# One product between the two forms of each weight sum in the last projection

## The chip, the cores and the metric

The kernel runs on one core of a Trainium2 chip (trn2). A core has a matrix engine (TensorE, in the profile PE, with PEld for its weight loads), a vector engine (VectorE, DVE), an activation engine (ScalarE, ACT), a general engine (GpSimd, POOL) and an engine that mostly issues transfers (SyncE, SP). Each engine works through its own list of instructions in order, and they wait for each other by semaphores. The metric is the device time of one execution in microseconds (us), lower is better.

## The reference, cut to what matters

Two layers on 512 tokens of width 1024. Only the end of the second layer and the final norm bear on the change:

```
def mla_layer(x, cos, sin, norm_g, w_in, ..., w_out):
    ...
    o = causal_mla_attention(q_nope, q_rope, k_nope, k_rope, v)
    y = o.reshape(B, S, MLA_WIDTH) * jax.nn.silu(z)      # 512 x 2048
    return x + y @ w_out                                 # w_out 2048 x 1024
...
    return rmsnorm(x, final_norm)
```

All is float32, and the sums must be accurate to that.

## The kernel before

Every product of two float32 matrices is made of three matmuls: both operands are split into a high and a low half, and `mm3` (lines 181 to 185) adds high x high (L183), then one low x high (L184) and the other (L185). The high half is an ACT copy (L166, L188, L559), the low half a DVE subtraction that reads the high one (L167, L189, L560).

The last projection, y @ w_out, is cut in 2 x 2 blocks and done by the scheme of Strassen and Winograd, with seven block products in place of eight. The gated attention result `y` is cut by tokens and by rows of the contraction into `a11, a12, a21, a22` (each 128 partitions x 8 x 256), the weights by contraction half (0 or 1) and by columns (`LEFT`, `RIGHT`). A product has 48 matmuls of 128 x 512: two strips of the weight block (`q` = 0, 1), two token tiles (`t` = 0, 1), four blocks of the contraction (`k`), three matmuls each. `multiply` goes through q, then t, then k.

The weight sums are made in place, by transfers that add to what lies there. `x_sum` has eight tiles `b_x` of 256 KB, `y_sum` four tiles `b_y` of 512 KB. A plain load is issued by SP (L548), an adding one by POOL (L546). `strip(i)` splits one half of the tiles into `w_hi` and `w_lo`. There are four buffers for those, so two strips at a time. An adding load into a tile can be issued only after the `w_lo` that reads the tile's old content.

The token side of a product goes into one of two slots: `slots[0]` is `a_hi_5948` and `a_lo_5949` in the rows below, `slots[1]` is `a_hi_5551` and `a_lo_5552`. `split_rows` fills a slot in two halves, `combine_rows` (L1055) adds or subtracts blocks of `y`, two DVE instructions per half.

The products collect in three pairs of PSUM banks: `acc` (`bank_5573`, `bank_5574`), `both` (`bank_6038`, `bank_6039`) and `last` (`bank_6040`, `bank_6041`). `gather` (L610, on DVE) adds a bank to the residual `xs`. A product that goes on in a bank can start only when the gather has read it. I name the products by their strips:

| product | token side | weight side | banks |
|---|---|---|---|
| first half | a11 | half 0, LEFT, a plain strip | acc |
| t1 | s1 = a21 - a22 | half 0, LEFT + RIGHT (`x_sum`) | both |
| p2 | a12 | half 1, LEFT (`y_sum`) | last |
| t2 | s2 = s1 - a11 | t1's sum + half 1, RIGHT (`x_sum`) | acc, going on |
| y1 | s2 + a12 | half 1, RIGHT (`y_sum`, a plain load) | both, going on |
| y2 | s3 = a11 - a21 | y1's block + half 0, RIGHT (`y_sum`) | acc, going on |
| t4 | a22 | t2's sum + half 1, LEFT (`x_sum`) | acc, going on |

The first of them runs between the last heads of the attention. `products()` writes out the order of t1 to y2 by hand, and `finish()` that of t4, the squares for the final norm (L1219 on ACT, `total` and `power` on POOL) and the stores. In both, `tc.manual_schedule()` keeps the order of the code on every engine.

Of the kernel before, what the change touches and what calls it, by code (L numbers as in the profile page):

```python
# [15 lines left out]
ALU = mybir.AluOpType  # L16
# [34 lines left out]
def trunk_kernel(  # L51
# [41 lines left out]
    def bank(dtype=F32):  # L93
        return ps.tile([P, 512], dtype, name="bank", tag="bank")
# [92 lines left out]
    def halves(src, hi, lo):  # L187
        act.activation(hi, src, AF.Copy)  # L188
        dve.tensor_tensor(lo, src, f32(hi), ALU.subtract)  # L189
# [51 lines left out]
    def start():  # L241
# [85 lines left out]
        for k in range(4):  # L327
            ready(0, k)
            products(0, k)
        w_lo(0, 4, 2)  # L330
        w_lo(1, 4, 2)
        ready(0, 4)
        products(0, 4)
        square(2)
        power(2)
        ready(0, 5)
        products(0, 5)
        ready(0, 6)
        scale(2)
# [194 lines left out]
    LEFT, RIGHT = slice(0, 512), slice(512, D)  # L534
# [35 lines left out]
    def quarters():  # L570

        return [
            [
                y[:, half * 8 + 2 * i : half * 8 + 2 * i + 2, t * 256 : (t + 1) * 256]
                for i in range(4)
            ]
            for t in range(2)
            for half in range(2)
        ]
# [9 lines left out]
    def part(o, wv, slot, q, t, start, stop, more, c=whole_row):  # L589

        for k in range(4):
            mm3(
                o,
                tuple(v[:, 4 * q + k, t * P : (t + 1) * P] for v in slot),
                tuple(v[:, k, c] for v in wv),
                start and k == 0,
                stop and k == 3,
                more=more,
            )

    def multiply(banks, strips, slot, start, then=None):
        for q in range(2):
            for t in range(2):
                part(banks[t], strips[q], slot, q, t, start and q == 0, q == 1, not start)
                if then and q == 1:
                    then(t)

    def gather(t, c, b, op=ALU.add):

        dve.tensor_tensor(xs[:, t, c], xs[:, t, c], b, op)  # L610


    a11, a12, a21, a22 = quarters()

    slots = [tuple(v[:, :, s * 256 : (s + 1) * 256] for v in (h_hi, h_lo)) for s in range(2)]
# [7 lines left out]
    x_sum, y_sum = Summed(w_out, 2), Summed(w_out, 2)  # L623
# [7 lines left out]
    acc = [bank() for _ in range(2)]  # L631
# [7 lines left out]
    both = [bank() for _ in range(2)]  # L639
# [23 lines left out]
    last = [bank() for _ in range(2)]  # L663
# [367 lines left out]
    def values(h):  # L1031
# [17 lines left out]
    a11, a12, a21, a22 = (  # L1049
        y[:, half * 8 : half * 8 + 8, t * 256 : (t + 1) * 256] for t in range(2) for half in range(2)  # L1050
    )

    def combine_rows(out, a, b, op, k0, k1):
        for k in range(k0, k1, 2):
            dve.tensor_tensor(*(v[:, k : k + 2, :] for v in (out, a, b)), op)  # L1055

    def split_rows(src, slot, k0, k1):
        halves(*(v[:, k0:k1, :] for v in (src, *slot)))
    x_sum, y_sum = Summed(w_out2, 1), Summed(w_out2, 2)
# [38 lines left out]
    first_half, slots = {}, {}  # L1098
    for h in range(H):
        p, odd = divmod(h, 2)  # L1100
        g, t = divmod(h + 5, 4)
        if h == 12:
# [3 lines left out]
            acc = [bank() for _ in range(2)]  # L1106
# [47 lines left out]
    s3, s2 = a21, a11  # L1154
    second_sum((("pt_hi", 1), ("pt_lo", 1)))
    both = [bank() for _ in range(2)]
    last = [bank() for _ in range(2)]
    g_fin = row(final_norm, D, "g_fin", tag="gain")

    def products():  # L1160

        combine_rows(s1, a21, a22, ALU.subtract, 6, 8)
        split_rows(s1, slots[0], 6, 8)
        x_sum.load(1, RIGHT, add=True, pieces=range(4))
        t1.append(x_sum.strip(1))
        x_sum.load(1, RIGHT, add=True, pieces=range(4, 8))
        multiply(both, t1, slots[0], True)
        split_rows(a12, slots[1], 0, 4)
        p2 = [y_sum.strip(0)]
        split_rows(a12, slots[1], 4, 8)  # L1170
        combine_rows(s3, a11, a21, ALU.subtract, 6, 8)
        combine_rows(s2, s1, a11, ALU.subtract, 6, 8)
        for t in range(2):
            gather(t, LEFT, acc[t])
        p2.append(y_sum.strip(1))
        y_sum.load(1, RIGHT)
        multiply(last, p2, slots[1], True)
        split_rows(s2, slots[0], 0, 4)
        split_rows(s2, slots[0], 4, 8)
        for t in range(2):  # L1180
            gather(2 + t, RIGHT, both[t])
        t2 = x_sum.strips()
        x_sum.load(1, LEFT, add=True)
        multiply(acc, t2, slots[0], False)
        for i in (0, 4):
            combine_rows(s2, s2, a12, ALU.add, i, i + 4)
            split_rows(s2, slots[1], i, i + 4)
        y1 = [y_sum.strip(0)]
        for t in range(2):
            gather(t, LEFT, last[t])  # L1190
        y1.append(y_sum.strip(1))
        y_sum.load(0, RIGHT, add=True)
        multiply(both, y1, slots[1], False)
        for t in range(2):
            gather(t, RIGHT, acc[t], ALU.subtract)
        split_rows(s3, slots[0], 0, 4)
        split_rows(s3, slots[0], 4, 8)
        for t in range(2):
            square(t, LEFT)
            total(t)  # L1200
        y2 = [y_sum.strip(0)]
        for t in range(2):
            gather(t, RIGHT, both[t])
        y2.append(y_sum.strip(1))
        for t in range(2):
            square(t, RIGHT)
            power(t)
        multiply(acc, y2, slots[0], False)
        split_rows(a22, slots[1], 0, 4)
        split_rows(a22, slots[1], 4, 8)  # L1210
# [6 lines left out]
    def square(t, c):  # L1217
        r = sm.tile([P, 1], F32, name="ssq", tag="ssq8", bufs=12)
        act.activation(  # L1219
            junk[:, : c.stop - c.start], xs[:, t, c], AF.Square, scale=D**-0.5, accum_out=r  # L1220
        )
        ssq[t].append(r)

    def total(t):

        r = sm.tile([P, 1], F32, name="total")
        pool.tensor_scalar(r, ssq[t][0], EPS, None, ALU.add)
        for q in ssq[t][1:]:
            pool.tensor_tensor(r, r, q, ALU.add)
        ssq[t] = [r]  # L1230

    def power(t):

        rs[t] = sm.tile([P, 1], F32, name="rs")
        pool.tensor_tensor(rs[t], ssq[t][1], ssq[t][0], ALU.add)
        pool.tensor_tensor(rs[t], rs[t], mhalf, ALU.pow)
# [92 lines left out]
```

## Time and profile before

| | |
|---|---|
| median of 3 runs | 716.93 us (716.78 to 717.99) |
| the profiled execution's own time | 715.48 us |
| its span in the profile | 713.6 us, so 1.9 us lie around it |
| PE busy | 700.9 us (98%) |
| DVE, ACT, POOL busy | 444.4, 347.5, 137.5 us |
| mean granted TensorE clock | 0.998 |
| t1 begins, the span ends | 639.25 us, 713.6 us |

The times in the rows are microseconds from the span's start. A row of the timeline has start, duration, engine, line, operation, output <- input, form and count, and in brackets how long the engine had been idle before it and what ended that. A matmul's end is modelled and overlaps the next one, so what counts is the distance from one start to the next.

### The profile page before, as it was taken

How to read it: one execution, taken by the hardware profiler on the slowest of the kernel's cores; microseconds unless marked ns; L12 is line 12 of the kernel's file. 1: busy time of each engine (PE TensorE's matmuls, PEld its weight loads, DVE VectorE, ACT ScalarE, POOL GpSimd, SP SyncE). 2: the span in 40 equal slices, each digit the busy share in tenths (PEclk: the TensorE clock that was granted, in tenths of full speed). 3: DMA queues.
4: the chain of work that ended last, by engine and by line, in shares of the span. 5: the costliest groups of instructions: out<-in, count | busy, mean ns of one | idle time of the engine just before them, and what ended most of it. 6: DMA issues, size and time to landing. Idle time of an engine off the chain costs nothing.

```text
span 713.6 us, 10044 instructions
## 1 busy us (share of the span) xinstructions
PE 700.9 (98%) x3529; PEld 600.6 (84%) x3529; DVE 444.4 (62%) x866; ACT 347.5 (49%) x748; POOL 137.5 (19%) x182
## 2 busy tenths in 40 slices
PE   8999999999999999999999999999999999999986
PEld 7988888888888888789888888898989898988875
DVE  5963452572486897750644220686676777699875
ACT  6452331341344465553652324756475477456662
POOL 5000000000001251064600006212221130122621
PEclk9999999999999999999999999999999999999999
DMA  8342323333245997334333433214122264378943
GB/s 259 105 144 73 118 83 94 104 84 108 89 148 144 235 192 136 96 86 129 99 117 103 118 97 101 78 27 108 52 65 70 79 163 132 65 172 212 153 84 119
DMA packets 69475, 82.79 MB, mean 116 GB/s; under 512 B 12080, under 2 KB 45872, under 8 KB 69424
## 3 DMA queue, kind: packets, MB, share of 16 engines
q1 hardware_dynamic: 60384, 65.10, 30.4%
q0 software_dynamic: 8896, 16.78, 13.8%
q8 instruction: 28, 0.46, 0.3%
q10 hardware_dynamic: 144, 0.26, 0.1%
q14 instruction: 23, 0.19, 0.1%
HBM read 75.83 MB, written 2.10 MB: 109 GB/s over the span
## 4 chain that ended last, share of the span: by engine, by line
PE 94%; DMA 2%; DVE 1%; issue 1%; ACT 1%; POOL 0%; POOLq 0%; SPq 0%; ACTq 0%; DVEq 0%
PE bank L184 28%; PE bank L183 28%; PE bank L185 28%; PE bank L1022 2%; PE bank L301 2%; PE bank L986 1%; PE bank L985 1%; DMA b_y<-in_mla_w_out 1%; PE bank L226 1%; PE bank L271 1%; PE bank L988 0%; PE bank L1044 0%; DMA xs<-in_x 0%; ACT junk L1219 0%; DVE a_lo L189 0%
## 5 line engine op out<-in xcount | busy, mean ns | idle before, releaser
L166 ACT ACTIVATE w_hi<-raw 128x512 fp32r<-128x512 f32 (+2 forms) x192 | 100.4, 576 | 135.6 <-PE bank L184 121.2
L167 DVE TENSOR_TENSOR w_lo<-raw,w_hi 128x512 fp32r<-128x512 f32 x124 | 81.7, 691 | 114.6 <-ACT w_hi L166 113.9
L183 PE MATMUL bank<-h_hi,w_hi 128*128 128x512 f32 x368 | 143.4, 390 | 0.0
L184 PE MATMUL bank<-h_hi,w_lo 128*128 128x512 f32 x368 | 143.2, 389 | 0.0
L185 PE MATMUL bank<-h_lo,w_hi 128*128 128x512 f32 x368 | 143.2, 389 | 0.0
L167 POOL TENSOR_TENSOR w_lo<-raw,w_hi 128x256 fp32r<-128x256 f32 (+2 forms) x68 | 61.4, 929 | 175.1 <-ACT w_hi L166 171.8
L185 PEld LDWEIGHTS bank<-h_lo,w_hi 128*128 128x128 f32 x368 | 69.1, 188 | 14.4
L184 PEld LDWEIGHTS bank<-h_hi,w_lo 128*128 128x128 f32 x368 | 69.1, 188 | 14.3
L183 PEld LDWEIGHTS bank<-h_hi,w_hi 128*128 128x128 f32 x368 | 69.1, 188 | 14.2
L183 PE MATMUL bank<-w_hi,h_hi 128*128 128x512 f32 (+1 forms) x176 | 64.6, 367 | 0.0
L185 PE MATMUL bank<-w_lo,h_hi 128*128 128x512 f32 (+1 forms) x176 | 64.1, 364 | 0.0
L184 PE MATMUL bank<-w_hi,h_lo 128*128 128x512 f32 (+1 forms) x176 | 64.1, 364 | 0.0
L183 PE MATMUL bank<-w_hi,a_hi 128*128 128x512 f32 (+1 forms) x116 | 44.7, 385 | 1.9 <-DVE xs L610 1.9
L185 PE MATMUL bank<-w_lo,a_hi 128*128 128x512 f32 (+1 forms) x116 | 44.5, 384 | 0.0
L184 PE MATMUL bank<-w_hi,a_lo 128*128 128x512 f32 (+1 forms) x116 | 44.4, 383 | 0.0
L183 PE MATMUL bank<-latT_hi,w_hi 128*128 128x512 f32 x104 | 42.4, 408 | 0.0
L184 PE MATMUL bank<-latT_hi,w_lo 128*128 128x512 f32 x104 | 40.6, 391 | 0.0
L185 PE MATMUL bank<-latT_lo,w_hi 128*128 128x512 f32 x104 | 40.6, 390 | 0.0
L559 ACT ACTIVATE w_hi<-b_x 128x512 fp32r<-128x512 f32 (+1 forms) x40 | 29.7, 794 | 19.4 <-DMA b_x<-in_pool_w_out 7.5
L546 POOL DMA_DIRECT2D b_x<-in_mla_w_out x24 | 21.5, 1399 | 81.4 <-DVE pt_lo L189 29.7
L560 DVE TENSOR_TENSOR w_lo<-b_x,w_hi 128x512 fp32r<-128x512 f32 (+1 forms) x40 | 34.0, 898 | 5.1 <-ACT w_hi L559 4.9
L185 PEld LDWEIGHTS bank<-w_lo,h_hi 128*128 128x128 f32 x176 | 33.0, 188 | 4.4
(204 smaller groups left out, 1417.8 us busy)
## 6 DMA issues: line engine op xcount, KB each, us to landing
raw<-in_pool_w_in SPq DMA_DIRECT2D x64, 256.0 KB, 3.2
raw<-in_mla_w_in SPq DMA_DIRECT2D x32, 256.0 KB, 3.2
b_x<-in_pool_w_out POOLq DMA_DIRECT2D x12, 512.0 KB, 7.6
b_x<-in_mla_w_out POOLq DMA_DIRECT2D x24, 256.0 KB, 6.3
raw<-in_mla_w_q_b SPq DMA_DIRECT2D x36, 128.0 KB, 2.4
raw<-in_pool_w_group SPq DMA_DIRECT2D x16, 256.0 KB, 2.6
q_r<-stack SPq DMA_DIRECT2D x64, 64.0 KB, 2.0
raw<-in_mla_w_kv_b SPq DMA_DIRECT2D x16, 256.0 KB, 3.0
```

The lines of the kernel that those rows point to most:

```text
L166: act.activation(hi, raw, AF.Copy)
L167: ins = eng.tensor_tensor(lo, raw, f32(hi), ALU.subtract)
L183: pe.matmul(o, a[0], b[0], start=start, stop=False, skip_group_check=more)
L184: pe.matmul(o, a[1], b[0], start=False, stop=False, skip_group_check=more)
L185: pe.matmul(o, a[0], b[1], start=False, stop=stop, skip_group_check=more)
L226: pe.transpose(pt[:, i * P : (i + 1) * P], xn[:, k * P : (k + 1) * P], ident)
L271: pe.transpose(pts[t // 2][k % 4][:, c : c + P], xn[t][:, k * P : (k + 1) * P], ident)
L301: pe.matmul(first[i][:, c], w0.views[0][a][:, k, i * P : (i + 1) * P], (h_hi, h_lo)[b][:, k, c], start=k == 0 and n == 0, stop=k == KD - 1 ...
L546: pool.dma_start(self.tiles[i], src, accum_op=ALU.add)
L559: act.activation(hv[:, k, :], raw, AF.Copy)
L560: eng.tensor_tensor(lv[:, k, :], raw, f32(hv[:, k, :]), ALU.subtract)
L1022: pe.transpose(b[:, n : n + P], pm[:, OFF[i] + j * P : OFF[i] + (j + 1) * P], ident)
```

## The change

The product y1 goes ahead of t2. The order was t1, p2, t2, y1, y2, t4, and is now t1, p2, y1, t2, y2, t4. So in `x_sum` two products lie from t1 to t2 (p2 and y1) and one from t2 to t4 (y2), and in `y_sum` none from p2 to y1 and one from y1 to y2 (t2). The sum s2 + a12 is now formed before t2 has used s2. It is therefore written over `a12` and not over `s2`, and goes to `slots[0]`, s2 to `slots[1]`. The gathers, the squares of tokens 0 to 255 and the loads move with their products.

```
         multiply(last, p2, slots[1], True)
-        split_rows(s2, slots[0], 0, 4)
-        split_rows(s2, slots[0], 4, 8)
+        n3 = a12
+        combine_rows(n3, s2, a12, ALU.add, 0, 4)
+        split_rows(n3, slots[0], 0, 4)
+        combine_rows(n3, s2, a12, ALU.add, 4, 8)
+        split_rows(n3, slots[0], 4, 8)
         for t in range(2):
             gather(2 + t, RIGHT, both[t])
+        y1 = y_sum.strips()
+        y_sum.load(0, RIGHT, add=True)
+        multiply(both, y1, slots[0], False)
+        split_rows(s2, slots[1], 0, 4)
+        split_rows(s2, slots[1], 4, 8)
+        for t in range(2):
+            gather(t, LEFT, last[t])
+            square(t, LEFT)
+            total(t)
         t2 = x_sum.strips()
         x_sum.load(1, LEFT, add=True)
-        multiply(acc, t2, slots[0], False)
-        for i in (0, 4):
-            combine_rows(s2, s2, a12, ALU.add, i, i + 4)
-            split_rows(s2, slots[1], i, i + 4)
-        y1 = [y_sum.strip(0)]
-        for t in range(2):
-            gather(t, LEFT, last[t])
-        y1.append(y_sum.strip(1))
-        y_sum.load(0, RIGHT, add=True)
-        multiply(both, y1, slots[1], False)
-        for t in range(2):
-            gather(t, RIGHT, acc[t], ALU.subtract)
+        multiply(acc, t2, slots[1], False)
         split_rows(s3, slots[0], 0, 4)
         split_rows(s3, slots[0], 4, 8)
         for t in range(2):
-            square(t, LEFT)
-            total(t)
+            gather(t, RIGHT, both[t])
         y2 = [y_sum.strip(0)]
         for t in range(2):
-            gather(t, RIGHT, both[t])
+            gather(t, RIGHT, acc[t], ALU.subtract)
         y2.append(y_sum.strip(1))
```

On DVE, behind the low half of p2's last weight tile (`b_y_6035`), there stood before the two halves of s2, the gathers from `both`, and t2's first tile:

```order
L560 TENSOR_TENSOR w_lo_6131<-b_y_6035,w_hi_6130 128x1024
L189 TENSOR_TENSOR a_lo_5949<-y_112,a_hi_5948 128x1024 x2
L610 TENSOR_TENSOR xs_76<-xs_76,bank_6038 128x512
L610 TENSOR_TENSOR xs_76<-xs_76,bank_6039 128x512
L560 TENSOR_TENSOR w_lo_6195<-b_x_5718,w_hi_6194 128x512
```

Now there stand the four additions for s2 + a12, each pair followed by its low half, then the gathers, and then y1's first tile (`b_y_6012`):

```order
L560 TENSOR_TENSOR w_lo_6131<-b_y_6035,w_hi_6130 128x1024
L1055 TENSOR_TENSOR y_112<-y_112 128x2x256 x2
L189 TENSOR_TENSOR a_lo_5949<-y_112,a_hi_5948 128x1024
L1055 TENSOR_TENSOR y_112<-y_112 128x2x256 x2
L189 TENSOR_TENSOR a_lo_5949<-y_112,a_hi_5948 128x1024
L610 TENSOR_TENSOR xs_76<-xs_76,bank_6038 128x512
L610 TENSOR_TENSOR xs_76<-xs_76,bank_6039 128x512
L560 TENSOR_TENSOR w_lo_6199<-b_y_6012,w_hi_6198 128x1024
```

The chain addition, high half, low half, twice over, has moved from before y1's strips to the same place one product earlier, and the two gathers now stand in it too. On POOL, the issues of the adding loads and the sums of squares stand like this against before:

```order
 L546 DMA b_x_5903<-in_mla_w_out 128x512
+L546 DMA b_y_6012<-in_mla_w_out 128x2x512
+L546 DMA b_y_6013<-in_mla_w_out 128x2x512
+L546 DMA b_y_6034<-in_mla_w_out 128x2x512
+L546 DMA b_y_6035<-in_mla_w_out 128x2x512
+L1227 TENSOR_SCALAR total_6269<-ssq_6267 128x1
+L1227 TENSOR_SCALAR total_6274<-ssq_6272 128x1
 L546 DMA b_x_5718<-in_mla_w_out 128x512
```

The four adding loads for y2 and two small sums now stand ahead of the eight adding loads for t4, which came first before. SP's list is the same row for row. On ACT, the two squares of tokens 0 to 255, left columns, now stand ahead of t2's first tile:

```order
L559 ACTIVATE w_hi_6204<-b_y_6035 128x1024
L188 ACTIVATE a_hi_5551<-y_112 128x1024 x2
L1219 ACTIVATE junk_6044,ssq_6267<-xs_76 128x512
L1219 ACTIVATE junk_6044,ssq_6272<-xs_76 128x512
L559 ACTIVATE w_hi_6276<-b_x_5718 128x512
```

Before, they stood ahead of y2's first tile:

```order
L559 ACTIVATE w_hi_6286<-b_y_6035 128x1024
L188 ACTIVATE a_hi_5948<-y_112 128x1024 x2
L1219 ACTIVATE junk_6044,ssq_6350<-xs_76 128x512
L1219 ACTIVATE junk_6044,ssq_6354<-xs_76 128x512
L559 ACTIVATE w_hi_6358<-b_y_6012 128x1024
```

They have moved one product earlier, with the gathers that they wait for.

## The prediction

> **What bounds the kernel now.** I read the busy shares first, then the waits of the stage that the change touches (640 us to the end), then the chain of waits there, then the starts of the matmuls, and last the lists of DVE and ACT around two places.
>
> ```profile
> PE 700.9 (98%) x3529; PEld 600.6 (84%) x3529; DVE 444.4 (62%) x866; ACT 347.5 (49%) x748; POOL 137.5 (19%) x182
> ```
>
> PE is the bound of the whole, so an order of the same matmuls can win only what PE waits. Of the waits from 640 us to 715 us two end at PE:
>
> ```profile
> PE bank L183 <- DVE xs L610: 1.9, 1, 1.9
> ...
> PEld bank L185 <- DVE w_lo L560: 0.4, 1, 0.4
> ```
>
> The timeline of PE has both, and the length of a product (start, duration, engine, line, form):
>
> ```profile
> 660.46 0.39 PE L183 MATMUL bank<-w_hi,a_hi 128*128 128x512 f32 x1
> ...
> 671.34 0.39 PE L183 MATMUL bank<-w_hi,a_hi 128*128 128x512 f32 x1
> 671.57 0.39 PE L184 MATMUL bank<-w_hi,a_lo 128*128 128x512 f32 x1
> 671.96 0.50 PE L185 MATMUL bank<-w_lo,a_hi 128*128 128x512 f32 x1
> 672.30 0.40 PE L183 MATMUL bank<-w_hi,a_hi 128*128 128x512 f32 x1
> ...
> 693.20 0.39 PE L185 MATMUL bank<-w_lo,a_hi 128*128 128x512 f32 x1
> 695.44 0.47 PE L183 MATMUL bank<-w_hi,a_hi 128*128 128x512 f32 x1 [1.85 <-DVE xs L610]
> 695.75 0.39 PE L184 MATMUL bank<-w_hi,a_lo 128*128 128x512 f32 x1
> ```
>
> 660.46 is the first matmul of t2 and 671.34 that of y1: 48 matmuls in 10.88 us, 0.227 us each. 695.44 is the first of t4; it was due at 693.20 + 0.23 = 693.43, so it is 2.01 late, and the next start comes 0.31 later instead of 0.23, 0.08 more. That is 2.09 us lost. y1's third matmul was due at 671.34 + 0.45 = 671.80, came at 671.96, and the next came 0.34 later: 0.16 + 0.11 = 0.27 us lost. Together 2.36 us: the most that the new order can win.
>
> The chain of waits says whence t4's wait comes:
>
> ```profile
> 677.04 9.45 DMA b_y<-in_mla_w_out
> ...
> 694.61 0.69 DVE xs L610
> ```
>
> The adding load of y2's last tile is issued when y1's low half has read it, lands 9.45 us later, at 686.49, and everything that ACT and DVE do next, up to the gather at 694.61 that t4 needs, is late by that.
>
> **The change: what goes.** y1 comes a product earlier, so the load for y2 is issued a product earlier, and t2 lies between. It is hidden by t2's 10.88 us: issued when y1's first low half ends (664.7 below), the last tile 3.5 later; with the 9.45 of before it lands near 678. ACT gets to it at 680.7 (it needs t2's first strip used up, so half of t2). If that cover failed by some time, t4 would be late by what exceeds the slack below.
>
> What is late next for t4 I take from the list of ACT, with its steps of before:
>
> ```profile
> 687.48 0.61 ACT L1219 ACTIVATE junk<-xs 128x512 f32<-128x512 f32 x1
> ...
> 688.85 2.00 ACT L188 ACTIVATE a_hi<-y 128x1024 fp32r<-128x1024 f32 x2
> 690.75 2.18 ACT L559 ACTIVATE w_hi<-b_x 128x512 fp32r<-128x512 f32 x4
> ```
>
> Two squares take 1.37, a22's high halves 1.90. In the new order y2's second strip is split from y2's first matmul on (its buffers are t2's): 1.95 for that, then 1.37 + 1.90, so a22 is done 5.2 after y2's start, t4's first strip can begin 5.4 after it (its buffers are y2's first strip's), and DVE's four low halves and the gather end about 9.8 after it. t4 is due at 10.88. So t4 waits for nothing, with 1.1 us to spare, and the whole 2.09 goes. The same for y1's 0.27: its place is taken by t2, whose first strip is ready 1.8 us early (below).
>
> **What comes.** Now the same chain that made y1 tight before, s2 + a12, stands right behind p2. Its rows on DVE, before:
>
> ```profile
> 655.10 2.35 DVE L189 TENSOR_TENSOR a_lo<-y,a_hi 128x1024 fp32r<-128x1024 f32 x2
> 657.38 1.28 DVE L610 TENSOR_TENSOR xs<-xs,bank 128x512 f32<-128x512 f32 x2
> 658.57 5.03 DVE L560 TENSOR_TENSOR w_lo<-b_x,w_hi 128x512 fp32r<-128x512 f32 x8
> 663.52 1.29 DVE L1055 TENSOR_TENSOR y<-y 128x512 f32<-128x512 f32 x2
> 665.93 1.22 DVE L189 TENSOR_TENSOR a_lo<-y,a_hi 128x1024 fp32r<-128x1024 f32 x1 [1.13 <-ACT a_hi L188]
> 667.08 1.28 DVE L1055 TENSOR_TENSOR y<-y 128x512 f32<-128x512 f32 x2
> 669.54 1.23 DVE L189 TENSOR_TENSOR a_lo<-y,a_hi 128x1024 fp32r<-128x1024 f32 x1 [1.19 <-ACT a_hi L188]
> 670.69 2.35 DVE L560 TENSOR_TENSOR w_lo<-b_y,w_hi 128x1024 fp32r<-128x1024 f32 x2
> ```
>
> and on ACT:
>
> ```profile
> 664.84 1.06 ACT L188 ACTIVATE a_hi<-y 128x1024 fp32r<-128x1024 f32 x1 [2.21 <-DVE y L1055]
> 668.45 1.06 ACT L188 ACTIVATE a_hi<-y 128x1024 fp32r<-128x1024 f32 x1 [2.55 <-DVE y L1055]
> 669.42 3.95 ACT L559 ACTIVATE w_hi<-b_y 128x1024 fp32r<-128x1024 f32 x4
> ```
>
> DVE and ACT wait for each other there: from the first addition to the first w_lo of y1 it is 670.69 - 663.52 = 7.17 us. ACT follows DVE by 0.03 each time and holds nothing else, so this chain won't be shorter in its new place. Before 655.10 nothing changes, and DVE goes from p2's last low half straight into it at 655.10. Behind it stand the two gathers from t1's banks, 658.57 - 657.38 = 1.19. So y1's first w_lo starts at 655.10 + 7.17 + 1.19 = 663.46. Before, the waiting matmul came 671.96 - 670.69 = 1.27 after that start: 664.73. y1 now begins where t2 began, at 660.46, and its third matmul, the first that reads w_lo, is due at 660.46 + 0.45 = 660.91. It is 3.82 late, and the restart costs 0.11 as before: 3.93 us lost. (ACT's high half of y1's first tile and the first gather, at about 662.1 and 662.9, lie inside this wait.) The next low half ends 1.17 after the first and is needed 1.4 after it (two contraction blocks of three matmuls), the third and fourth only with the second strip, 5.4 on: no further wait.
>
> y1's weights are there: its plain loads are unchanged on SP, the last issued at 655.6, landing in 5.4, so at 661.0; ACT, which begins y1's tiles 669.42 - 663.52 = 5.90 after 655.10 and takes 0.97 for each, reads the third tile at 662.9.
>
> ```profile
> 648.15 7.43 SPq L548 DMA_DIRECT2D b_y<-in_mla_w_out  x4
> ```
>
> t2 after it begins at 671.34 + 3.9 = 675.3. DVE comes from y1's four low halves (663.46 + 4.7), s2's halves 2.3 and two gathers 1.2, at 671.6; the two squares that now stand ahead of t2 on ACT run to 672.6; t2's first w_lo ends at 673.9, needed at 675.7. They are hidden with 1.8 us to spare, and each us beyond would be a us on the end.
>
> POOL's eight adding loads for t4 now stand behind y2's four and the two sums, but each also waits for t2's w_lo, so they go out from 674 to 682. Before they took this to land:
>
> ```profile
> b_x<-in_mla_w_out POOLq DMA_DIRECT2D x8, 256.0 KB, 8.0
> ```
>
> The last lands near 690. ACT wants the first four at 691.6 and the others at 697: hidden, the first by some 5 us.
>
> **The sum.** +3.93 - 0.27 - 2.09 = +1.57 us, on the profiled execution 715.48 + 1.57 = 717.05. That execution is 1.45 below the median of the runs; against the median it is 716.93 + 1.57 = 718.50. Bounds: the new wait is built of measured steps, 0.3 either way; t4's wait goes between not at all and wholly (0 to 2.09), and I take wholly, since the row that it hung on is early by 8 us. Another 0.3 is the drift of matmul starts behind a wait.
>
> **The rivals.**
>
> *The clock falls in the new wait.* From 660.9 to 664.7 PE has two matmuls only. The granted clock in these rows is the number behind the five engines' busy times, 1.00 and 0.54:
>
> ```profile
> 694.00:695.00 1.00, 0.00 (x0) 0.00 (x0) 1.00 (x3) 1.00 (x4) 0.00 (x0) 1.00 0.00 0
> ...
> 711.00:712.00 1.00, 0.00 (x0) 0.00 (x0) 0.00 (x0) 0.00 (x0) 0.00 (x0) 0.54 1.02 383
> ```
>
> The old 2.0 us gap left the clock at 1.00; behind the last matmul (near 706.7) it fell only at about 711.1, after 4.4 us. The new wait has no empty stretch above 2.1 us, since y1's first two matmuls run when the gather lets them, which speaks against it. Half the clock over the 2.5 us that the record still shows would cost 1.25 us: 719.8. [...]
>
> *t4 still waits.* The adding loads of t4 go out 8 to 15 us later than before, with y2's just ahead of them. If they took twice the 8.0, the first four would land near 692 and t4 would keep most of its 2.09: 720.5. For it: adding loads were slow one after the other before. Against: they have the queue to themselves after 678.
>
> *Not slower after all: the landing is worse in the runs than in the profile.* The median is 1.45 us above the profiled execution. If that sits in the landing of y2's tiles, the only place here where PE hangs on a transfer, the change takes it off as well: 718.50 - 1.45 = 717.05, no change. It decides for faster when the landing is over 3.0 us worse than in the profile (1.57 + 1.43). For it: those loads took 9.45. Against: nothing says where the 1.45 lies.
>
> **How the numbers follow.** About 0.2% (1.43 us) is what a measurement of this kernel can tell from no change, and my sum is just over it. My forecast has 0.66, its own range 717.9 to 719.2, a bit more than half of it slower by over 0.2%, the rest within. The clock has 0.08, t4's wait 0.09, the landing 0.17 (0.11 within, 0.06 faster). Slower: 0.38 + 0.17 = 0.55; same: 0.28 + 0.11 = 0.39; faster 0.06. The range 716.9 to 720.3 holds the times of all three rivals but one, t4's wait, and cuts a tail of the others.
>
> **What would show it.** Right: y1's third matmul waits for DVE's w_lo near 664.7 with some 3.8 us of PE idle before; t4's first matmul comes 0.23 after y2's last, near 697.0; the adding loads of y2 are in the chain of waits no more; the chain of DVE from 655.1 has the same 7.2 + 1.2 us. Wrong: PE idle under 2.2 us at y1 (then no slower), a wait at t4, t2 or y2 of 0.5 us or more, or a granted clock under 1.00 between 660 and 670.

## The result and the profile after

The changed kernel takes 719.01 us (median of 15 runs, 717.18 to 720.82), the kernel before, run beside it on the same chip, 716.93 us (15 runs, 715.30 to 718.53). The ratio is 1.0026, its 95% interval 1.0016 to 1.0036: slower by 2.1 us. The profiled execution of the changed kernel took 719.61 us, its span is 717.8 us and the mean granted clock 0.991, against 715.48, 713.6 and 0.998 before. So the two profiled executions lie 4.1 us apart, twice the distance of the medians. That difference is half of the story below.

The page of the changed kernel has the same work in it, at nearly the same share:

```profile
PE 701.5 (98%) x3529; PEld 600.8 (84%) x3529; DVE 444.5 (62%) x866; ACT 347.2 (48%) x748; POOL 138.0 (19%) x182
```

Of the waits after 640 us, these now end at PE. The numbers are total, count and longest:

```profile
PEld bank L183 <- ACT w_hi L559: 2.9, 1, 2.9
PE bank L183 <- ACT w_hi L559: 2.5, 1, 2.5
...
PEld bank L185 <- DVE w_lo L560: 1.2, 1, 1.2
...
PE bank L185 <- DVE w_lo L560: 0.5, 1, 0.5
```

The wait for `xs`, t4's, is gone, and waits at y1, put down to `w_hi` and `w_lo`, have come. PE's timeline at y1, at the start of t2 (677.97) and at the start of t4 (699.73):

```profile
660.42 0.39 PE L185 MATMUL bank<-w_lo,a_hi 128*128 128x512 f32 x1
663.29 0.69 PE L183 MATMUL bank<-w_hi,a_hi 128*128 128x512 f32 x1 [2.48 <-ACT w_hi L559]
663.78 0.63 PE L184 MATMUL bank<-w_hi,a_lo 128*128 128x512 f32 x1
664.94 0.80 PE L185 MATMUL bank<-w_lo,a_hi 128*128 128x512 f32 x1 [0.52 <-DVE w_lo L560]
665.53 0.63 PE L183 MATMUL bank<-w_hi,a_hi 128*128 128x512 f32 x1
...
670.22 0.39 PE L185 MATMUL bank<-w_lo,a_hi 128*128 128x512 f32 x1
670.45 0.40 PE L183 MATMUL bank<-w_hi,a_hi 128*128 128x512 f32 x1
...
677.97 0.39 PE L183 MATMUL bank<-w_hi,a_hi 128*128 128x512 f32 x1
...
699.50 0.39 PE L185 MATMUL bank<-w_lo,a_hi 128*128 128x512 f32 x1
699.73 0.39 PE L183 MATMUL bank<-w_hi,a_hi 128*128 128x512 f32 x1
```

Read the starts. The third matmul of y1 comes at 664.94. t4 follows y2's last matmul by 0.23 and waits for nothing. But behind the wait the starts lie 0.43 apart instead of 0.23, until about 670.2. t2 begins at 677.97. With y1's other 45 matmuls at 0.227 each it would have begun at 664.94 + 0.34 + 45 x 0.227 = 675.5: 2.5 us are lost to this pace. The windows of one microsecond name its cause. The granted clock is the number after the busy times of PE, PEld, DVE, ACT and POOL:

```profile
661.00:662.00 1.00, 0.00 (x0) 0.00 (x0) 0.68 (x1) 1.00 (x2) 0.00 (x0) 1.00 0.00 0
662.00:663.00 1.00, 0.00 (x0) 0.00 (x0) 1.00 (x2) 1.00 (x2) 0.00 (x0) 1.00 0.00 0
663.00:664.00 1.00, 0.71 (x2) 0.43 (x2) 1.00 (x3) 1.00 (x2) 0.00 (x0) 0.69 0.00 0
664.00:665.00 1.00, 0.48 (x2) 0.07 (x1) 1.00 (x2) 1.00 (x3) 0.00 (x0) 0.50 0.00 0
...
669.00:670.00 1.00, 1.00 (x4) 0.81 (x3) 1.00 (x2) 0.00 (x0) 1.00 (x1) 0.50 1.12 203
```

PE is empty in two whole windows, and then the clock is at half. DVE and ACT over the same stretch have the chain that PE waits for:

```profile
655.29 1.29 DVE L1055 TENSOR_TENSOR y<-y 128x512 f32<-128x512 f32 x2
657.71 1.23 DVE L189 TENSOR_TENSOR a_lo<-y,a_hi 128x1024 fp32r<-128x1024 f32 x1 [1.13 <-ACT a_hi L188]
658.85 1.29 DVE L1055 TENSOR_TENSOR y<-y 128x512 f32<-128x512 f32 x2
661.32 1.23 DVE L189 TENSOR_TENSOR a_lo<-y,a_hi 128x1024 fp32r<-128x1024 f32 x1 [1.18 <-ACT a_hi L188]
662.47 1.28 DVE L610 TENSOR_TENSOR xs<-xs,bank 128x512 f32<-128x512 f32 x2
663.66 4.62 DVE L560 TENSOR_TENSOR w_lo<-b_y,w_hi 128x1024 fp32r<-128x1024 f32 x4
...
661.20 3.88 ACT L559 ACTIVATE w_hi<-b_y 128x1024 fp32r<-128x1024 f32 x4
```

From the first addition to the first `w_lo` it is 663.66 - 655.29 = 8.37 us, against the 7.17 + 1.19 = 8.36 forecast. The row of y1's first matmul (663.29) names `w_hi`, but the high half that this matmul reads is the first of ACT's four and done by 662.3. The second, done at 663.19, it doesn't need: in the kernel before, y1 began at 671.34 and its second high half was done only at 671.41. What did end just before 663.29 is the first of the two gathers from t1's banks, at 663.15. So the first two matmuls of y1 wait for the gather, and the third for `w_lo`.

In all, the profiled pair differs by 4.2 us of span: 0.2 because t1 began later (639.44 instead of 639.25), before the change has done anything, 2.5 from the clock, and the other 1.5 from the waits, where 1.57 was forecast. Since t1's start differs from execution to execution, I compare below what lies behind it: the time from t1's first matmul to the span's end, "the end part" from here on. It is 74.35 us before and 78.36 after.

### The profile page after: what moved, and what is told of

Read it like the earlier page. It is cut to its first block, busy times and chain, and to the rows that moved or that the text cites. A ratio compares the mean times of both kernels' runs of the same rounds, so it can differ in the third digit from the quotient of the medians.

```text
span 717.8 us, 10049 instructions
## 1 busy us (share of the span) xinstructions
PE 701.5 (98%) x3529; PEld 600.8 (84%) x3529; DVE 444.5 (62%) x866; ACT 347.2 (48%) x748; POOL 138.0 (19%) x182
## 4 chain that ended last, share of the span: by engine, by line
PE 93%; DVE 3%; issue 1%; ACT 1%; DMA 0%; POOL 0%; POOLq 0%; SPq 0%; DVEq 0%; ACTq 0%
PE bank L184 28%; PE bank L183 28%; PE bank L185 28%; PE bank L1022 2%; PE bank L301 2%; PE bank L986 1%; PE bank L985 1%; DVE w_lo L560 1%; DVE y L1055 1%; PE bank L226 1%; PE bank L1044 0%; PE bank L988 0%; DVE xs L610 0%; DMA xs<-in_x 0%; ACT a_hi L188 0%
## 5 line engine op out<-in xcount | busy, mean ns | idle before, releaser
L183 PEld LDWEIGHTS bank<-w_hi,h_hi 128*128 128x128 f32 x176 | 33.1, 188 | 4.4
```

The costliest lines, as they stand in the source:

```text
L183: pe.matmul(o, a[0], b[0], start=start, stop=False, skip_group_check=more)
```

## The experiments

All share the question which part of the +2.1 us is the wait, which the clock, and why the medians differ by less than the profiles. Theory: the wait at y1 costs what was summed, the clock costs some 2 us on top, and the kernel before is in its usual run worse than in its profile. Rival: only one of these, the rest being the spread.

### The empty stretch filled

The changed kernel, and eleven matmuls into a spare bank where PE has nothing to do, between p2 and y1:

```
         y_sum.load(0, RIGHT, add=True)
+        spare, hi = bank(), slots[1][0]
+        for i in range(11):
+            pe.matmul(spare, hi[:, i % 8, :P], ..., start=True, stop=True)
         multiply(both, y1, slots[0], False)
```

> The changed kernel with 11 matmuls of 128x512 put between p2 and y1 on PE. They read a_hi of slots[1], write a spare bank that nobody reads, and at 0.227 us each fill 2.5 us of the 3.8 us in which PE waits for y1's first low half. Theory (wait plus clock): the wait itself stays, y1's third matmul still comes near 664.9, but the granted clock stays at 1.00 from 660 to 672, so the 2.4 us that y1's matmuls lost at half clock come back: span 715.2 to 715.6 in place of 717.8, mean clock 0.997 or above in nearly every execution, median about 717.3. Rival (the wait alone costs it, and the low clock is a chance of that one execution): the median stays at 719.0. Rival (the clock falls for a reason other than an idle PE): it falls here too, between 663 and 670.

Measured: 716.96 us (12 runs, 715.95 to 718.12), ratio to before 1.0003 (0.9990 to 1.0016), before 717.09 in the runs beside it. One of its windows, where the changed kernel ran at half clock, and then its timeline of PE:

```profile
665.00:666.00 1.00, 0.86 (x4) 0.73 (x5) 1.00 (x2) 1.00 (x2) 0.62 (x1) 1.00 0.00 0
```

```profile
660.86 2.65 PE L1189 MATMUL bank<-a_hi 128*128 128x512 f32 x11
663.50 0.47 PE L183 MATMUL bank<-w_hi,a_hi 128*128 128x512 f32 x1
663.80 0.40 PE L184 MATMUL bank<-w_hi,a_lo 128*128 128x512 f32 x1
665.14 0.50 PE L185 MATMUL bank<-w_lo,a_hi 128*128 128x512 f32 x1 [0.94 <-DVE w_lo L560]
```

The wait is still there: the third matmul comes at 665.14, with t1 0.2 later than in the changed kernel. The clock stays at 1.00 and the pace is 0.23 again. The end part is 75.86 us, 1.51 above the 74.35 of before, where the sum of waits was 1.57. So eleven matmuls that compute nothing take 2.05 us off the median (719.01 to 716.96). The clock's part is shown, though one expectation failed: the mean clock is 0.997 or above in four of the twelve runs only. The profile, with 0.992, has a mean clock of 0.71 from 5 to 13 us and of 0.85 from 13 to 20, at the kernel's start, and 1.00 from 640 to 706, so the mean clock of a run doesn't tell where it fell. But the wait's +1.5 is not in the median at all: 716.96 against 717.09. The kernel before must lose about as much somewhere that its first profile does not show.

### The wait shortened

Two versions of the changed kernel that only reorder the new chain. The first puts both pairs of additions ahead of both splits, so that DVE no longer stands idle for ACT's high halves; the second also splits only half of the token side before the gathers and y1's first strip:

```
         combine_rows(n3, s2, a12, ALU.add, 0, 4)
-        split_rows(n3, slots[0], 0, 4)
         combine_rows(n3, s2, a12, ALU.add, 4, 8)
+        split_rows(n3, slots[0], 0, 4)
         split_rows(n3, slots[0], 4, 8)
         ... gathers
         y1 = y_sum.strips()
```

```
         combine_rows(n3, s2, a12, ALU.add, 0, 4)
-        split_rows(n3, slots[0], 0, 4)
         combine_rows(n3, s2, a12, ALU.add, 4, 8)
-        split_rows(n3, slots[0], 4, 8)
+        split_rows(n3, slots[0], 0, 4)
         ... gathers
-        y1 = y_sum.strips()
+        y1 = [y_sum.strip(0)]
+        split_rows(n3, slots[0], 4, 8)
+        y1.append(y_sum.strip(1))
```

The first of them:

> The changed kernel with one swap: all four additions for s2 + a12 stand ahead of the two splits, so DVE adds the second half while ACT copies the first. Theory: the chain in front of y1 loses the 1.13 and 1.18 us in which DVE waited for ACT, the wait of y1's third matmul shrinks from 3.8 to about 1.5 us, too short for the clock to fall, and t4 does not wait: 1.6 - 2.36 = -0.7 us against before, span 712.9, ratio 0.998 to 0.999. Rival (the chain is bound by DVE's work, not by the turns between the two engines): the wait stays above 3 us and the ratio at 1.002 or above.

Measured: 714.70 us (12 runs, 714.31 to 715.67), ratio 0.9975 (0.9964 to 0.9985), end part 73.67. Its third matmul in y1, due at 660.50 (y1 was due at 660.05, and 0.45 is two matmuls), is 1.5 us late, as expected:

```profile
661.99 0.51 PE L185 MATMUL bank<-w_lo,a_hi 128*128 128x512 f32 x1 [0.94 <-DVE w_lo L560]
```

The second:

> The changed order of products, but in front of y1 all four additions for s2 + a12 come first, then only the first half of the slot is split, then the gathers and y1's first strip, then the slot's second half and y1's second strip. Theory: y1's first w_lo can start at 655.1 + 2.5 + 1.15 + 1.2 = 660.0 in place of 663.5, y1's third matmul comes at 661.3 and is 0.3 to 0.4 late in place of 3.8, the clock stays at 1.00, t4 does not wait: 0.4 - 2.36 = -2.0 us against the kernel before, span about 711.7, ratio about 0.997. Rival (DVE as a whole is the bound of this stage, and the time comes back as waits at t2, y2 or t4): less than 1 us gained against before, ratio 0.999 or above.

Measured: 712.97 us (6 runs, 712.53 to 713.91), ratio 0.9952 (0.9934 to 0.9971), end part 72.33. On DVE the four additions now run without a pause, and the first `w_lo` of y1 starts 658.98 - 654.22 = 4.76 us after the first of them instead of 8.37:

```profile
654.22 2.50 DVE L1055 TENSOR_TENSOR y<-y 128x512 f32<-128x512 f32 x4
656.64 1.23 DVE L189 TENSOR_TENSOR a_lo<-y,a_hi 128x1024 fp32r<-128x1024 f32 x1
657.78 1.28 DVE L610 TENSOR_TENSOR xs<-xs,bank 128x512 f32<-128x512 f32 x2
658.98 2.35 DVE L560 TENSOR_TENSOR w_lo<-b_y,w_hi 128x1024 fp32r<-128x1024 f32 x2
```

PE goes into y1 nearly without a wait:

```profile
659.58 0.39 PE L183 MATMUL bank<-w_hi,a_hi 128*128 128x512 f32 x1
659.80 0.39 PE L184 MATMUL bank<-w_hi,a_lo 128*128 128x512 f32 x1
660.25 0.51 PE L185 MATMUL bank<-w_lo,a_hi 128*128 128x512 f32 x1
```

Both end parts moved as the steps say: -0.68 and -2.02 against 74.35. So the new wait is the chain of additions and splits. The medians gained more, -2.4 and -4.1 us. The excess, 1.7 and 2.1 us, is about the 1.6 that the filled kernel showed, so it must sit in what the three are compared with, the kernel before. The second version is the best of all that ran: 0.48% faster than before and, by the medians, 0.84% faster than the changed kernel.

### Where the kernel before loses more than its profile shows

Two places could do it: the landing of y2's adding loads, and t4's wait with what follows it. First, t4's wait shortened. The kernel before, with the two squares and `power` of the right columns moved behind t4's first strip, which takes 1.4 us of ACT out of the chain that t4 waits for:

```
-        for t in range(2):
-            square(t, RIGHT)
-            power(t)
         multiply(acc, y2, slots[0], False)
...
         t4 = [x_sum.strip(0)]
+        for t in range(2):
+            square(t, RIGHT)
+            power(t)
```

> The kernel before, with one move: the two squares of tokens 0 to 255, right columns, and the powers behind them stand behind t4's first strip on ACT and no more ahead of a22's split. It prices t4's wait by itself. Theory: t4's wait of 2.0 us is ACT and DVE time behind the late landing of y2, so without the 1.37 us of squares it shrinks to about 0.8 us: -1.2 us, span 712.4, ratio 0.998. Rival (the landing alone sets the gather's time): no change, ratio 1.000.

Measured: 715.31 us (12 runs, 713.96 to 717.17), ratio 0.9977 (0.9963 to 0.9990), end part 74.16. The median moved by 1.8, the end part by only 0.19 against the first profile. The reason stands in ACT's list, in the row of y2's first tile:

```profile
678.95 1.06 ACT L559 ACTIVATE w_hi<-b_y 128x1024 fp32r<-128x1024 f32 x1 [3.32 <-DMA b_y<-in_mla_w_out]
```

That is 40.71 us after t1's first matmul. In the first profile of before it is 39.71, in the same order of the loads:

```profile
678.96 1.06 ACT L559 ACTIVATE w_hi<-b_y 128x1024 fp32r<-128x1024 f32 x1 [2.32 <-DMA b_y<-in_mla_w_out]
```

The landing came 1 us later, in the experiment or in the usual run. To tell, two more profiles of the kernel before:

> The kernel before, unchanged, for a second profile. Theory L: y2's first tile reaches ACT more than 39.7 us after t1's first matmul, or its last more than 47.3 us after it, and PE waits longer at y2 and t4 than the 2.0 us of the first profile: the stretch from t1 to the end is 75 to 76.5 us. Theory C: the landings are as in the first profile, and the granted clock falls below 1.00 between 690 and 702. Rival (the start): the stretch is 74.3 to 74.5 us at full clock, and t1 begins later than 639.25.

> The same as b1_before, a third profile: which of landing, clock behind t4's wait, and start differs from the first profile, by the same three marks.

Measured: 715.64 and 715.47 us. y2's first tile reaches ACT 40.77 and 40.58 us after t1, the end parts are 75.46 and 75.25. In the first of them PE now waits in y2 as well:

```profile
684.03 0.50 PE L185 MATMUL bank<-w_lo,a_hi 128*128 128x512 f32 x1 [0.35 <-DVE w_lo L560]
...
695.65 0.47 PE L183 MATMUL bank<-w_hi,a_hi 128*128 128x512 f32 x1 [2.25 <-DVE xs L610]
```

So the early landing was the exception of the first profile. Against the mean of these two end parts, 75.36, the moved squares gained 1.20.

Second, the clock behind t4's wait. The kernel before, and eight matmuls into a spare bank between y2 and t4:

```
         multiply(acc, y2, slots[0], False)
+        spare, hi = bank(), slots[0][0]
+        for i in range(8):
+            pe.matmul(spare, hi[:, i, :P], ..., start=True, stop=True)
         split_rows(a22, slots[1], 0, 4)
```

> The kernel before with 8 matmuls of 128x512 (1.8 us) between y2 and t4 on PE, into a bank that nobody reads, in the stretch of 2.0 us in which PE waits for t4's gather. The timed runs of the kernel before are some 1.5 us above its profiled execution, and the new order seems to be rid of that. Theory C (the clock falls behind t4's wait in many executions): filled, it doesn't, and the median falls by 1 us or more, ratio 0.998 or below. Theory L (the landing of y2's four adding loads is later in most executions than in the profiled one): the fill changes nothing, ratio 1.000. Either way the profiled execution has the clock at 1.00 from 640 to 705.

Measured: 716.40 us (12 runs, 715.30 to 717.00) against 717.39, ratio 0.9985 (0.9975 to 0.9994), end part 75.66. The ratio lies between what the two theories expected, and its interval leaves out the 1.000 of the landing alone. No work is taken off and t4's gather comes as late as before, yet the median gains 1.0 us, while the end part of its one profile is 0.3 above 75.36. So in the usual run something behind that wait costs about 1 us that a busy PE avoids. The mean clocks point to the clock: 0.9965 over these runs, 0.9949 over those of the kernel before, and the difference over 716 us is 1.1 us.

Third, all that hangs on the landing taken away. The adding loads of half 0, RIGHT, are left out, so y2 multiplies by y1's block alone:

```
         y1.append(y_sum.strip(1))
-        y_sum.load(0, RIGHT, add=True)
         multiply(both, y1, slots[1], False)
```

> The kernel before without the four adding loads for y2, so that y2 multiplies y1's weight block again (the half 0, RIGHT part of the sum is left out, and the result with it). The order of everything else stays. Theory L or C (what the timed runs lose beyond the profile hangs on the landing): PE waits at neither y2 nor t4, the stretch from t1's first matmul to the end is 72.2 to 72.5 us in place of 74.35, and the median falls by 3.5 to 4 us, to about 713.3. Rival (the extra lies elsewhere, at the start of the kernel for one): the stretch shrinks just so, but the median by 2.1 us only, to 715.0.

Measured: 713.93 us (6 runs, 713.16 to 714.75), ratio 0.9956 (0.9941 to 0.9971), so 3.5 us less; end part 72.68 (72.2 to 72.5 expected), which is 1.67 below the first profile of before and 2.68 below 75.36.

At this point the half clock behind t4's wait was only inferred, since none of the three profiles of before had it. Three more profiles of that kernel, and one of the changed one:

> The kernel before, unchanged, a further look, for one question: does the granted clock fall behind t4's wait in executions that are longer than 716 us? Theory (clock behind t4's wait): an execution of 716.5 us or more shows the clock at 0.5 for some us after about 695, matmul starts 0.43 us apart there, and t1's first matmul to the span's end takes 76.3 to 77.5 us instead of 74.35 to 75.5; one near 715.5 shows 1.00 there. Rival (the long executions lose at the start of the kernel alone): the clock falls only between 5 and 20 us, t1 begins at 639.3 or later, and the part from t1 on takes at most 75.5 us in every execution.

> The kernel before, unchanged, as the look before it and with the same question: half clock behind t4's wait (t1 to the end 76.3 to 77.5 us), or only at the kernel's start (t1 at 639.3 or later, 75.5 us at most from there).

> The kernel before, unchanged, third look, same question: half clock behind t4's wait (t1 to the end 76.3 to 77.5 us), or only at the kernel's start (t1 at 639.3 or later, 75.5 us at most from there).

> The changed kernel, unchanged, a second look. Theory: the half clock behind y1's wait is the rule and not the accident of one profile: the clock is at 0.5 from about 663 to 670 again, t1's first matmul to the span's end takes 78.4 us, the mean clock is at most 0.994. Rival (the first profile was an accident): the clock is 1.00 there, and it takes 75.9 us as with the empty stretch filled.

Measured: 716.88, 717.91 and 718.71 us for the kernel before, 717.66 us for the changed one. All three long executions of before have the half clock behind t4's wait. The windows of the first of them:

```profile
694.00:695.00 1.00, 0.00 (x0) 0.00 (x0) 1.00 (x3) 1.00 (x3) 0.00 (x0) 1.00 0.00 0
695.00:696.00 1.00, 0.64 (x2) 0.57 (x3) 1.00 (x3) 0.81 (x3) 0.00 (x0) 0.54 0.00 0
696.00:697.00 1.00, 1.00 (x4) 0.81 (x3) 1.00 (x3) 0.76 (x3) 0.88 (x1) 0.50 0.00 0
697.00:698.00 1.00, 1.00 (x3) 0.77 (x3) 1.00 (x3) 0.00 (x0) 1.00 (x1) 0.50 0.00 0
698.00:699.00 1.00, 1.00 (x5) 0.75 (x4) 1.00 (x3) 0.00 (x0) 0.30 (x1) 0.75 0.00 0
```

and its t4, where the starts go from 0.23 apart to 0.43:

```profile
692.73 0.39 PE L185 MATMUL bank<-w_lo,a_hi 128*128 128x512 f32 x1
695.36 0.77 PE L183 MATMUL bank<-w_hi,a_hi 128*128 128x512 f32 x1 [2.24 <-DVE xs L610]
696.35 0.63 PE L185 MATMUL bank<-w_lo,a_hi 128*128 128x512 f32 x1
697.63 0.63 PE L185 MATMUL bank<-w_lo,a_hi 128*128 128x512 f32 x1
```

The gap is the same as in two executions where the clock stayed at 1.00: 2.24 us empty here, 2.25 in the profile quoted further up (and 1.85 in the first profile, which kept its clock too). So the same gap costs the clock in one execution and not in another: in three of six here, three of five with the long gap. What decides is not shown; what was measured of it stands in the last section. The end parts of the three are 76.87, 76.85 and 77.14, in the mean 1.6 above 75.36. The rival, that long executions lose only at the kernel's start, falls. In part it holds too: t1 begins between 638.13 and 639.76 us in the six, and the clock falls between 5 and 20 us in two of them (0.79 in the mean from 5 to 13 us in the first of the long executions, 0.71 in the third), as in five of the eight profiles of the other versions. But the two don't go together: the earliest t1, 638.13, belongs to the one with 0.79. What moves t1 by 1.6 us stays open.

The second profile of the changed kernel has the half clock again, but later and half as long. Its windows:

```profile
664.00:665.00 1.00, 1.00 (x5) 0.76 (x6) 1.00 (x2) 1.00 (x2) 0.92 (x1) 0.89 0.00 0
665.00:666.00 1.00, 1.00 (x4) 0.81 (x3) 1.00 (x2) 0.88 (x1) 0.84 (x2) 0.50 0.00 0
...
668.00:669.00 1.00, 1.00 (x6) 0.83 (x5) 1.00 (x2) 0.00 (x0) 1.00 (x1) 0.91 1.08 195
```

Its end part is 77.55, which is 1.69 above the filled kernel's 75.86; the expected 78.4 was too much. Its mean clock is 0.993, and 13 of the changed kernel's 15 runs have that or less, but so have five of the filled kernel's twelve, the profiled one from a fall at the kernel's start. In the mean the two differ by 0.9923 to 0.9949, 1.9 us over 716. So the clock costs the changed kernel 1.7 or 2.5 us in the two profiles, and the medians say 2.05.

### The account

Against the usual end part of before without a fall of the clock, 75.36, the kernels stand like this. The last column is what the median moved beyond the end part, in us; before's median is that of the runs beside it, 717.09 or, for the last two, 717.39. Each end part is that of one profile:

| kernel | end part - 75.36 | median - before's median | beyond |
|---|---|---|---|
| changed, stretch filled | +0.50 | -0.13 | -0.6 |
| additions first | -1.69 | -2.39 | -0.7 |
| additions first, half split | -3.03 | -4.12 | -1.1 |
| no adding load | -2.68 | -3.46 | -0.8 |
| before, t4's gap filled | +0.30 | -0.99 | -1.3 |

The five have no fall of the clock in their end part, and each gains 0.6 to 1.3 more than its end part says, 0.9 in the mean. This fits the kernel before paying 1.6 us behind t4's wait in about half of its executions, as three of its six profiles did. The moved squares leave 0.6 beyond in the same way (-1.20 and -1.78). The changed kernel itself: +0.50, -0.9, and 2.05 for its own clock, together +1.65, against a measured +2.08. The 0.4 left over is within what a ratio of two medians here is uncertain by (an interval of 0.1% either way is 0.7 us). The 2.05 is itself the step from one of these medians to another, so this sum tests the 0.9 only.

## Why the prediction was right, and where it was not

The forecast was 718.5 with a range of 716.9 to 720.3 and slower by over 0.2% as the likeliest; 719.01 came. The number is near by luck: two terms that the sum left out, -1.9 and +2.05, nearly cancel in it.

**The new wait at y1: right.** Third matmul forecast at 664.73, measured 664.94, of which 0.19 is t1's later start. The two versions with a shorter chain moved as its steps say.

**t4's wait and y1's old tightness: right as rows, too small as a gain.** t4 follows y2 by 0.23, as forecast, and y2's loads left the chain. But the 2.09 was the price of t4's wait in one execution with the earliest landing of all those seen. In the usual run the landing is 1.0 later, which makes y2 and t4 wait longer, and t4's wait is followed by a half clock about every second time. The term that was mis-sized is "the whole 2.09 goes": what went is about 2.1 + 1.0 + 0.9. The 1.0 is the third rival's mechanism, which had 0.17; the 0.9 is another, which no rival named for the old wait. That rival said 717.05, and the filled kernel, in which no clock falls at y1, gave 716.96, so it had the size right and half of the cause.

**The clock in the new wait: wrong.** It had a chance of 0.08, and it happens in both profiles of the changed kernel; the medians and the mean clocks above say that it is the rule. The step that failed is the argument from the two old rows. "The old 2.0 us gap left the clock at 1.00" was true of that execution, and of two more with a longer gap, and false of three others with that longer gap. The 4.4 us read at the end of the kernel was no threshold. And "no empty stretch above 2.1 us" was wrong too: the stretch was 2.6 us (660.65 to 663.29). The prediction's own rows had it: the first gather was to start at 655.10 + 7.17 = 662.27 and takes 0.68, so y1, due at 660.46, could not begin before 662.95, 2.5 us later. The price of 1.25 us was too low; it is 1.7 or 2.5. Added up from the windows' clocks, the half-clock spells are 3.42 us in each of the last three profiles of before, and 6.82 and 3.40 in the first and the second of the changed kernel; the 1.25 stood for 2.5 us at half clock. And 2.24 us of empty PE was followed by such a spell in three of five executions.

**The rest that was costed at nothing: right.** t2, y2 and t4 wait for nothing in the changed kernel. On ACT, y2's tiles are now ready before their buffers are, and their rows wait for PE and no longer for a transfer:

```profile
683.38 2.01 ACT L559 ACTIVATE w_hi<-b_y 128x1024 fp32r<-128x1024 f32 x2 [1.35 <-PE bank L184]
688.82 2.01 ACT L559 ACTIVATE w_hi<-b_y 128x1024 fp32r<-128x1024 f32 x2 [3.43 <-PE bank L184]
```

So the sign and the size came out, since +1.57 as summed, -1.9 that the kernel before pays beyond its profile (1.0 landing, 0.9 clock) and +2.05 for the clock make +1.7. Forecasting from one profile, I had no way to see the -1.9, but its own 1.45 us below the median was the sign that something was missing, and I gave it a place among the rivals only, not in the sum.

## What to carry to other kernels

A gap on TensorE had two prices here, its own length and the spell at half clock that followed it in some executions, and the second was more than half of the first (2.5 beside 3.9 us at y1, 1.6 beside 2.4 at t4). Matmuls into a spare bank told them apart and took the second away: eleven took 2.05 us off the median at y1, eight took 1.0 off at t4. Where the profiled execution lies below the median by as much as the change is worth, look at more executions of the kernel before, since the wait that you price may be the lucky one. And when a product is moved forward, ask which of its preparation could be put first: here the same reordering goes from 0.26% slower to 0.25% faster with the four additions ahead of the splits, and to 0.48% faster when half of the split also waits.

## What the runs showed of the hardware

The same gap between the same matmuls, 2.24 us by the rows (2.40 from 0.23 behind the last start to the next), led to half clock in three executions and not in two others. The fall began 2.1 to 5.2 us after PE ran empty (695.08 after 692.96 in the first of the three long executions, 664.78 after 659.56 in the second profile of the changed kernel, where the starts had come 0.23 to 0.34 apart again since 663.84).

The moments at which the clock changes can be read from the rows of one microsecond. Two more of these, from the second profile of the changed kernel:

```profile
9.00:10.00 1.00, 0.82 (x5) 0.82 (x6) 0.86 (x3) 0.07 (x1) 0.06 (x1) 0.71 1.07 357
...
712.00:713.00 1.00, 0.00 (x0) 0.00 (x0) 0.13 (x1) 0.10 (x1) 0.00 (x0) 0.78 0.04 14
```

A mean of 0.71 says that the clock was at half for the last 0.58 us of that microsecond, so it fell at 9.42. In the same way it fell at 664.78 (0.89, quoted further up) and at 712.56. From the first to the second it is 655.36 us, and from there to the third 47.78. In the first profile of the changed kernel it fell at 11.44 (0.72 in the mean from 11 to 12 us), at 663.38 (0.69, quoted further up) and at 714.58 (0.79 from 714 to 715): 651.94 and 51.20 us apart. The shortest spells at half clock are 3.40 to 3.42 us, and the four distances are 192, 14, 191 and 15 times 3.413. So the gap's length may not be all that counts, but also its place against these moments: that was not tried, and what decides is not shown. The gaps of all eight profiles of the two kernels, each from 0.23 behind the last start to the next start, with the time from its beginning to the fall and the length of the spell (all in us):

| profile | gap | from its beginning to the fall | at half clock |
|---|---|---|---|
| before, the first | 2.01 | no fall | 0 |
| before, the second | 2.41 | no fall | 0 |
| before, the third | 2.40 | no fall | 0 |
| before, 716.88 us | 2.40 | 2.12 | 3.42 |
| before, 717.91 us | 2.40 | 2.73 | 3.42 |
| before, 718.71 us | 2.41 | 3.18 | 3.42 |
| changed, the first | 2.64 | 2.73 | 6.82 |
| changed, the second | 2.64, and 1.10 two matmuls later | 5.22 | 3.40 |

In the first profile of the changed kernel y1's wait for `w_lo` lies behind the fall (0.52 by its row), and the spell is twice as long as the others. The table holds for these matmuls of 128x512. The falls at the kernel's start were not worked out.

The four adding loads of y2 landed 1 us earlier in one profile than in the seven others with the same order: counted from t1, the first of them reached ACT at 39.71, against 40.56 to 40.92. Why was not tried.
